# A new order for the token mixer of a hybrid encoder block: contiguous weight loads, projections between the transposes, scan constants after the norms, the Fourier work two rounds earlier, and another last filler

## The chip, the cores and the metric

The kernel runs on one core of a Trainium2 chip. The metric is the device time of one launch in microseconds (us). Engines are named as the profile names them: PE is TensorE (matmuls; PEld its weight loads), DVE is VectorE, ACT is ScalarE, POOL is GpSimd, SP is SyncE, which here only issues DMAs.

## The reference

One encoder layer on x of 512 positions by 1024, all in float32:

```python
h = rmsnorm(x, norm1_g)
z = h @ w_in                                  # 512 x 1024
# columns 0..511: S5 group, 32 channel groups of 16, 64 complex states, scans forward and backward
y = s5_scan(u, fwd) + s5_scan(u, bwd, reverse=True) + ssm_d * u
y = gelu(y);  y_ssm = y * sigmoid(y @ w_glu)
# columns 512..1023: Fourier group, 4 groups of 128 channels
f = real(fft2(f, axes=(positions, channels), norm="ortho"));  y_fno = einsum("sgc,gcd->sgd", f, w_fourier)
x = x + concat(y_ssm, y_fno) @ w_out
h = rmsnorm(x, norm2_g)
x = x + peer_ffn(h, w_query, sub_keys, expert_u, expert_v)   # 8 heads, 128 x 128 experts, top 16
out = rmsnorm(x, final_g)
```

The change touches the first half, the token mixer (the lines down to `x + concat @ w_out`), and the layout of w_query.

## The kernel before, in words

The instructions of each engine run in the order in which the program writes them (a hand-written schedule); engines wait for each other by semaphores, and a tile with `bufs=n` can be written again only when its n-th predecessor has been read. Float32 products are made as three matmuls of split operands (`mm3`: high x high, high x low, low x high). `split` makes the two parts: ACT copies the high part (line 108, tiles `whi`, `hTh`, `ygh`), DVE or POOL subtracts it to get the low part (line 109, `wlo`, `hTl`, `ygl`).

The mixer has three stretches.

- **Front.** x is loaded as four row tiles `xt`, each is normed (`normed`: square and sum on ACT, root, reciprocal and scaling on DVE, line 151), transposed on PE and split into `hTh` and `hTl` (`turned_parts`). w_in is loaded in eight column blocks of 512 KB (`w_raw`), three buffers deep. `zT(zp[q], w[q], columns)` makes the projection of S5 channel block q, `z_fourier(g, …)` that of Fourier block g. At the same time DVE, ACT and POOL build the scan constants: rotation tables by doubling (`turns(m)`, a complex product `cmul` of six operations; m = 5 is on POOL), powers `pw`, and from them `pi`, `pv`, `kap` and `ck`.
- **Loop of rounds.** The S5 group has eight blocks n of four channel groups. Block n needs, in this order: `weights_in(n)` (POOL, tile `win`), `turned_in(n)` (PE transposes, line 419), `weights_out(n)` (DVE tile `v`, ACT copies `bb`, `rc`, `sg` from `rot`), `kernels(n)` (PE, line 431), `toeplitz(n)` (DMA there and back), `states_in(n)` (PE), `scan(n)` (DVE, eight operations that end in tile `sx`) and `states_out(n)` (PE, lines 495 and 497). Round n of `for n in range(7)` scans block n on DVE while PE does filler: the Fourier projections `z_fourier` in rounds 0 to 3, then the Fourier transform (`columns`, `table`, `rows`) one round behind the other, so that `rows(i, c)`, 12 matmuls of 512 columns each, fills rounds 4 to 6.
- **Tail.** After the loop `scan(7)` runs on DVE beside a last filler on PE, `rows(3, 0)` and `rows(3, 1)`, 24 matmuls. Then come `states_out(7)`, the GLU product (`glu`), the product with w_out (`wo_part(i, k)`: row tile i, block k of the mix; blocks 4 to 7 are the Fourier half), its eight weight blocks loaded in turn through the three `raw` buffers, norm2 and the transposes for the query stage, which starts at about 266 us of the span.

From there PE is busy almost without a gap to the end, so a shift of the mixer's end shifts the end of the kernel.

Of the kernel before, what the change touches and what calls it, by code (L numbers as in the profile page):

```python
# [22 lines left out]
TC = 8  # L23
# [45 lines left out]
def build(ctx, tc, A, dbg=None, stop=None):  # L69
# [215 lines left out]
    def turns(m, gs, eng=None):  # L285
# [6 lines left out]
    for m in range(1, 5):  # L292
        turns(m, slice(0, G))
    for h in range(2):
        gs = slice(h * G // 2, (h + 1) * G // 2)
        turns(5, gs, ge)
    pw = sp.tile([128, 2, TC + 1, G], FT, name="pw")
    ve.memset(pw[:, 0, 0], 1.0)
    ve.memset(pw[:, 1, 0], 0.0)
# [9 lines left out]
    zp = [acc_bank() for _ in range(4)]  # L309
    w = []  # L310
    for i in range(NT):
        normed(xt[i], xt[i], g1, sw.tile([128, D], mybir.dt.bfloat16, tag="cm", name="scr"))
        if i:
            turned_parts(xt[i - 1], hTh, hTl, i - 1)
            w.append(w_parts(raws[i - 1], ge))
    se.activation(warm, eps, AF.Gelu)
    for q in range(2):
        zT(zp[q], w[q], slice(0, 256))


# [15 lines left out]
    pv = sc.tile([128, 3, TC + 1, G], FT, name="pv")  # L336
    for c, (src, sign) in enumerate(((0, 1.0), (1, -1.0), (0, -1.0))):
        se.activation(pv[0:64, c], pw[0:64, src], AF.Copy, scale=sign)
        se.activation(pv[64:128, c], pw[64:128, src, ::-1], AF.Copy, scale=sign)
# [12 lines left out]
    ck = sc.tile([128, 2, G, CG], FT, name="ck")  # L352
    shp = [128, G, CG]
    cmul(ck[:, 0], ck[:, 1], cre, cim, bc(kap[:, 0, :, None], shp), bc(kap[:, 1, :, None], shp), shp)
    pro.close()
# [257 lines left out]

    for n in range(7):
        if n % 2 == 0 and n < 6:
            inputs(n // 2 + 1)
        if n == 2:
            fourier_load()
        if n == 3:
            table_load(0)  # L620
            table_load(1)
        if n == 0:
            z_fourier(0, w, range(0, 4))
# [4 lines left out]
        if n < 2:  # L628
            raws.append(w_raw(6 + n))
        if n + 2 < 8:  # L630
            weights_in(n + 2)
        if 0 < n < 3:
            z_fourier(n, w, range(0, 4))
        elif n == 3:
            z_fourier(n, w, range(0, KD))
# [4 lines left out]
        elif n:  # L640
            rows(n - 4, 0)
# [4 lines left out]
        if n > 3:  # L646
            table(n - 3, 0)
        if n < 3:
            z_fourier(n, w, range(4, 8))
            w = w_parts(raws[n + 1])  # L650
        elif n > 3:
            rows(n - 4, 1)
            table(n - 3, 1)
            if n < 6:
                table_load(n - 2)
        if n >= 3:
            columns(n - 3)
        if n == 3:
            table(0, 0)
            table(0, 1)  # L660
# [21 lines left out]
    def wo_raw(k):  # L682
        raw = blk.tile([128, 1024], FT, tag="raw", bufs=3, name="raw")
        nc.sync.dma_start(raw, A["w_out"][k * 128:(k + 1) * 128])
        return raw
# [627 lines left out]
```

## Time and profile before

| | us |
|---|---|
| median of three timed runs | 1533.1 (1532.39 to 1537.7) |
| profiled execution, its own time | 1530.49 |
| span of that execution | 1528.7 |
| PE busy in the span | 1462.2 (96%) |
| DVE, ACT, POOL busy | 1288.4, 719.1, 819.2 |
| mean granted TensorE clock | 0.990 |

The span runs from the first to the last instruction of the core. A granted clock of 1 stands for 2.4 GHz, 0.5 for 1.2 GHz. In the rows below an instruction is named by its line, its engine, the tile that it writes, an arrow and the tiles that it reads; "x8" says that a row stands for eight of them in a run, and a bracket gives the engine's idle time before it and what ended that.

### The profile page before, as it was taken

The numbers are of one execution on the slowest core, as the hardware profiler recorded it, in microseconds if no ns is written. First come the engines' busy times: TensorE is split into PE (matmuls) and PEld (weight loads), VectorE is DVE, ScalarE is ACT, GpSimd is POOL, SyncE is SP. The second block draws the span as 40 slices with busy tenths as digits, with TensorE's granted clock in tenths as the row PEclk, the third lists the DMA queues.
The fourth block names the chain that finished last, engine by engine and source line by source line (L and its number), as shares of the span: only waits on it lengthen the run. The fifth ranks groups of instructions, "written<-read, shape, count | busy, mean of one in ns | idle before, by whom it ended". The sixth has DMA issues, their size and how long they took to land.

```text
span 1528.7 us, 22444 instructions
## 1 busy us (share of the span) xinstructions
PE 1462.2 (96%) x8045; PEld 1320.9 (86%) x8045; DVE 1288.4 (84%) x2156; ACT 719.1 (47%) x1332; POOL 819.2 (54%) x482
## 2 busy tenths in 40 slices
PE   1799999999998999999999999999999999999997
PEld 1678878889998999999999888888888888888885
DVE  7889744799999999988773997888888888889886
ACT  5245544334445777777773433333333333333333
POOL 5446722336795776777775544544544454444530
PEclk9899999999998999999999999999999999999999
DMA  6233353323585999999999888898888888998883
GB/s 139 69 94 84 114 175 86 97 83 124 182 297 194 327 333 295 328 327 334 329 329 357 319 293 306 326 335 323 308 306 320 321 298 318 332 337 309 299 298 111
DMA packets 205951, 388.13 MB, mean 254 GB/s; under 512 B 27152, under 2 KB 127248, under 8 KB 205712
## 3 DMA queue, kind: packets, MB, share of 16 engines
q1 hardware_dynamic: 102896, 209.86, 40.8%
q0 software_dynamic: 36864, 134.23, 24.7%
q10 hardware_dynamic: 66080, 42.61, 8.7%
q8 instruction: 63, 1.03, 0.3%
q14 instruction: 48, 0.39, 0.1%
HBM read 341.46 MB, written 45.19 MB: 253 GB/s over the span
## 4 chain that ended last, share of the span: by engine, by line
PE 78%; DVE 10%; DMA 3%; ACT 3%; issue 2%; POOL 1%; ACTq 1%; SPq 0%; POOLq 0%; DVEq 0%
PE mm L103 10%; PE mm L101 10%; PE mm L102 10%; PE acc L103 9%; PE acc L102 9%; PE acc L101 9%; PE acc L1092 5%; PE misc L103 4%; PE misc L101 4%; PE misc L102 4%; DVE one L1018 1%; PE mm L431 1%; ACT hot L1078 1%; PE misc L1180 1%; DMA gd<-stg 1%
## 5 line engine op out<-in xcount | busy, mean ns | idle before, releaser
L109 POOL TENSOR_TENSOR wlo<-raw,whi 128x1024 fp32r<-128x1024 f32 x153 | 388.3, 2540 | 511.8 <-ACT whi L108 470.9
L108 ACT ACTIVATE whi<-raw 128x1024 fp32r<-128x1024 f32 x288 | 304.6, 1059 | 345.4 <-PE misc L103 201.9
L101 PE MATMUL mm<-h2h,whi 128*128 128x384 f32 (+2 forms) x1168 | 403.1, 345 | 0.2 <-ACT h2h L163 0.2
L103 PE MATMUL mm<-h2h,wlo 128*128 128x384 f32 (+2 forms) x1168 | 396.6, 340 | 0.4 <-POOL wlo L109 0.4
L102 PE MATMUL mm<-h2l,whi 128*128 128x384 f32 (+2 forms) x1168 | 396.3, 339 | 0.3 <-DVE h2l L164 0.3
L838 DVE TENSOR_TENSOR pre<-pre,gb 128x384 f32<-128x384 f32 x128 | 182.5, 1426 | 53.2 <-ACT pre L888 24.6
L101 PEld LDWEIGHTS mm<-h2h,whi 128*128 128x128 f32 x1168 | 220.6, 189 | 5.8 <-ACT h2h L163 0.5
L102 PEld LDWEIGHTS mm<-h2l,whi 128*128 128x128 f32 x1168 | 220.6, 189 | 5.9 <-DVE h2l L164 0.5
L103 PEld LDWEIGHTS mm<-h2h,wlo 128*128 128x128 f32 x1168 | 220.1, 188 | 5.2 <-POOL wlo L109 0.8
L109 DVE TENSOR_TENSOR wlo<-raw,whi 128x1024 fp32r<-128x1024 f32 x135 | 169.9, 1258 | 55.2 <-ACT whi L108 54.2
L101 PE MATMUL acc<-whi,ah 128*128 128x512 f32 x512 | 199.4, 389 | 1.4 <-ACT ah L108 1.4
L102 PE MATMUL acc<-wlo,ah 128*128 128x512 f32 x512 | 200.2, 391 | 0.4 <-DVE wlo L109 0.3
L103 PE MATMUL acc<-whi,al 128*128 128x512 f32 x512 | 200.3, 391 | 0.0
L1144 POOL DMA_INDIRECT row<-in_expert_v_dram,ei x128 | 171.5, 1340 | 40.1 <-issue 18.2
L1154 DVE SCALAR_TENSOR_TENSOR gscr<-row,hnat 128x1024 bf16<-128x1024 f32 x128 | 183.7, 1435 | 6.0 <-DMA row<-in_expert_u_dram,ei 5.0
L1162 DVE SCALAR_TENSOR_TENSOR x<-row,pr,x 128x1024 f32<-128x1024 f32 x128 | 184.7, 1443 | 1.3
L1144 POOL DMA_INDIRECT row<-in_expert_u_dram,ei x128 | 163.5, 1277 | 29.4 <-issue 17.0
L888 ACT ACTIVATE pre<-mm 128x384 f32<-128x384 f32 x128 | 62.3, 487 | 185.9 <-PE mm L103 182.4
L1066 DVE TENSOR_TENSOR hot<-iota,tT 128x1024 f32<-128x1024 f32 x96 | 113.6, 1215 | 29.2 <-PE acc L1092 20.7
L1078 ACT ACTIVATE hot<-hot,tT 128x128 f32<-128x128 f32 x384 | 117.8, 390 | 0.0
L101 PEld LDWEIGHTS acc<-whi,ah 128*128 128x128 f32 x512 | 96.2, 188 | 21.1 <-ACT ah L108 2.1
L103 PEld LDWEIGHTS acc<-whi,al 128*128 128x128 f32 x512 | 96.1, 188 | 20.8 <-DVE al L109 0.8
(308 smaller groups left out, 2207.5 us busy)
## 6 DMA issues: line engine op xcount, KB each, us to landing
raw<-in_expert_uT_dram SPq DMA_DIRECT2D x128, 512.0 KB
raw<-in_expert_v_dram SPq DMA_DIRECT2D x128, 512.0 KB
gd<-stg ACTq DMA_DIRECT2D x24, 1024.0 KB
gb<-gd SPq DMA_DIRECT2D x64, 384.0 KB
pre_d<-pre ACTq DMA_DIRECT2D x78, 192.0 KB
pre<-pre_d SPq DMA_DIRECT2D x78, 192.0 KB
raw<-in_w_query_dram SPq DMA_DIRECT2D x16, 512.0 KB
raw<-in_w_in_dram SPq DMA_DIRECT2D x8, 512.0 KB
```

Of the source, the lines that this page charges most:

```text
L101: te.matmul(ps, lhsT=ah, rhs=bh, start=first, stop=False)
L102: te.matmul(ps, lhsT=ah, rhs=bl, start=False, stop=False)
L103: te.matmul(ps, lhsT=al, rhs=bh, start=False, stop=last)
L108: se.activation(hi, raw, AF.Copy)
L109: ins = (eng or ve).tensor_tensor(lo, raw, hi.bitcast(FT), OP.subtract)
L838: ve.tensor_tensor(pt, pt, gb[:, :, b % IG], OP.mult)
L1066: ve.tensor_tensor(hot, bc(iota[:, None, None, :128], shp), bc(tT[:, 0:2, t0:t0 + 4, None], shp), OP.is_equal)
L1078: se.activation(hot[:, 0, a], hot[:, 0, a], AF.Copy, scale=tT[:, 2, t0 + a:t0 + a + 1])
L1092: te.matmul(ps[:, a * 128:(a + 1) * 128], lhsT=hot[:, 1, a], rhs=hot[:, 0, a], start=True, stop=True)
L1144: ge.indirect_dma_start(out=row[:, :], out_offset=None, in_=A[table], in_offset=bass.IndirectOffsetOnAxis(ap=ei[:, m:m + 1], axis=0))
L1154: ve.scalar_tensor_tensor(scr, rows.pop(n), 1.0, hnat, op0=OP.mult, op1=OP.mult, accum_out=pr[:, m:m + 1])
L1162: ve.scalar_tensor_tensor(x[i], rows.pop(n), pr[:, m:m + 1], x[i], op0=OP.mult, op1=OP.add)
```

## The change

The order of the mixer is written anew; what is computed stays.

- **Loads.** `blocks()` lays out w_in and w_query on the host so that a column block is contiguous: 4 KB in a row per partition where it was eight pieces of 512 B. norm1_g, which was broadcast by DMA to 128 partitions (512 KB), is loaded as one row of 4 KB and spread by two PE matmuls with a row of ones into two PSUM banks `gb1`; `norm1(i)` scales in two halves of 512 from there. The order of the first loads changes, ssm_b moves ahead of the third block.
- **Front.** The seeds of `rot` are copied by POOL (12 copies) where ACT did it. The square's scratch tile has the tag `tm`, not `cm`, which the rotations on DVE use too. Ahead of the norms only `turns(1)` and `turns(2)` are left; `turns(3)`, `ck`, `turns(4)`, `pv` come after the fourth transposes, and POOL's `turns(5)` in two halves behind `weights_in(0)` and `weights_in(1)`, where it ran at 15 to 34 us. The projections stand between transposes.
- **Loop.** `z_fourier(0)` is done whole ahead of the loop, 1 and 2 in round 0, 3 in round 1; `columns`, `table` and `rows` stand two rounds earlier, so that `rows` fills rounds 2 to 5. Round 6 has no Fourier filler; the splits of the Fourier result (`mfh`, `mfl`) and the loads of w_out blocks 4 and 5 are there now.
- **Tail.** The last filler, ahead of `states_out(7)`, is `wo_part` of blocks 4 and 5 for row tiles 0 and 1, 24 matmuls as well.

```diff
     def w_raw(c):
         raw = blk.tile([128, 1024], FT, tag="raw", bufs=3, name="raw")
-        nc.sync.dma_start(raw.rearrange("p (k c) -> p k c", k=KD),
-                          A["w_in"][:, c * 128:(c + 1) * 128].rearrange("(k p) c -> p k c", p=128))
+        nc.sync.dma_start(raw, A["w_in"][c])
...
+    gb1 = [mm_bank() for _ in range(2)]
+    for f in range(2):
+        te.matmul(gb1[f], lhsT=g1[:, D:], rhs=g1[:, f * 512:(f + 1) * 512], start=True, stop=True)
...
-            se.activation(rot[:, c, :, 2 ** m], csn[:, c, 1 + m], AF.Copy)
+            ge.tensor_copy(rot[:, c, :, 2 ** m], csn[:, c, 1 + m])
...
+    def norm1(i):
+        r = rstd_of(sumsq(xt[i], sw.tile([128, D], mybir.dt.bfloat16, tag="tm", name="scr")))
+        for f in range(2):
+            fs = slice(f * 512, (f + 1) * 512)
+            ve.scalar_tensor_tensor(xt[i][:, fs], xt[i][:, fs], r, gb1[f], op0=OP.mult, op1=OP.mult)
...
+    norm1(0)
+    norm1(1)
+    turn1(0)
+    w = [w_parts(raws[0], ge)]
+    powers()
+    turn1(1)
+    norm1(2)
+    w.append(w_parts(raws[1], ge))
+    zT(zp[0], w[0], h0)
...
+    weights_in(0)
+    w.append(w_parts(raws[3]))
+    raws.append(w_raw(4))
+    inputs(0)
+    zT(zp[1], w[1], h1)
+    z_ssm(1, zp[1])
+    turns(3)
+    shp = [128, G, CG]
+    cmul(ck[:, 0], ck[:, 1], cre, cim, bc(kap[:, 0, :, None], shp), bc(kap[:, 1, :, None], shp), shp)
...
+    turns(4)
+    pro.close()
+    turns(5, slice(0, G // 2), ge)
+    zT(zp[2], w[2])
+    w.append(w_parts(raws[4]))
...
     kernels(0)
     toeplitz(0)
+    z_fourier(0, w[4], range(0, KD))
+    turns(5, slice(G // 2, G), ge)
     weights_out(1)
...
+        if n == 0:
+            z_fourier(1, w[5], range(0, KD))
+        elif n == 1:
+            z_fourier(3, w[7], range(0, KD))
...
+        elif n < 6:
+            rows(n - 2, 0)
...
         if n == 6:
+            for g in range(4):
...
+                se.activation(h, fstate["acc"][g], AF.Copy)
+                ve.tensor_tensor(l, fstate["acc"][g], h.bitcast(FT), OP.subtract)
...
+            wr = {k: wo_raw(k) for k in (4, 5)}
...
     scan(7)
-    wr = {k: wo_raw(k) for k in (4, 5)}
     wo = {k: wo_parts(wr[k], ge) for k in (4, 5)}
-    rows(3, 0)
-    rows(3, 1)
-    fac = fstate["acc"]
+    po = {i: [acc_bank() for _ in range(2)] for i in range(2)}
+    for k in (4, 5):
+        for i in range(2):
+            wo_part(i, k, k == 4, False)
```

POOL, from the constants to the first input weights. Before, `turns(5)` (`gm` and `rot`, here its last two operations) and the zeroing of small tiles stand ahead of the low parts of w_in and of `win`:

```order
L222 TENSOR_TENSOR rot<-rot 128x16x31
L223 TENSOR_TENSOR rot<-gm,rot 128x16x31
L303 MEMSET bb_229 128x384
L303 MEMSET bb_230 128x384
L306 MEMSET us_233 128x8
L307 MEMSET us_233 128x8
L306 MEMSET us_234 128x8
L307 MEMSET us_234 128x8
L109 TENSOR_TENSOR wlo<-raw,whi 128x1024 x3
L384 TENSOR_TENSOR win<-ssm_b,pi 128x1024
```

The same place on POOL in the changed kernel:

```order
L109 TENSOR_TENSOR wlo<-raw,whi 128x1024 x3
L399 TENSOR_TENSOR win<-ssm_b,pi 128x1024
L400 TENSOR_TENSOR gm<-ssm_b,pi 128x1024
L401 TENSOR_TENSOR win<-win,gm 128x1024
L217 TENSOR_TENSOR gm<-rot 128x496
L218 TENSOR_TENSOR rot<-rot 128x16x31
L219 TENSOR_TENSOR rot<-gm,rot 128x16x31
L220 TENSOR_TENSOR gm<-rot 128x496
L221 TENSOR_TENSOR rot<-rot 128x16x31
L222 TENSOR_TENSOR rot<-gm,rot 128x16x31
```

The first half of `turns(5)` has moved behind the first `win`; the second half stands behind the second `win` in the same way.

DVE, from the constants to the first output weights. Before, `ck` is followed by the low part of a w_in block (`wlo`) and block 0's `v`:

```order
L222 TENSOR_TENSOR ck<-ssm_c,kap 128x512
L223 TENSOR_TENSOR ck<-cm,ck 128x512
L109 TENSOR_TENSOR wlo<-raw,whi 128x1024
L384 TENSOR_TENSOR v<-ck,pv 128x1152
L385 TENSOR_TENSOR cm<-ck,pv 128x1152
L386 TENSOR_TENSOR v<-v,cm 128x1152
L109 TENSOR_TENSOR wlo<-raw,whi 128x1024
L436 TENSOR_TENSOR kf<-kf 16x4x16
```

The same place on DVE in the changed kernel:

```order
L222 TENSOR_TENSOR ck<-cm,ck 128x512
L217 TENSOR_TENSOR cm<-rot 128x480
L218 TENSOR_TENSOR rot<-rot 128x32x15
L219 TENSOR_TENSOR rot<-cm,rot 128x32x15
L220 TENSOR_TENSOR cm<-rot 128x480
L221 TENSOR_TENSOR rot<-rot 128x32x15
L222 TENSOR_TENSOR rot<-cm,rot 128x32x15
L109 TENSOR_TENSOR wlo<-raw,whi 128x1024
L399 TENSOR_TENSOR v<-ck,pv 128x1152
L400 TENSOR_TENSOR cm<-ck,pv 128x1152
L401 TENSOR_TENSOR v<-v,cm 128x1152
L109 TENSOR_TENSOR wlo<-raw,whi 128x1024
```

The six operations of `turns(4)` (and, ahead of `ck`, those of `turns(3)`) now stand between the fourth norm and block 0's `v`.

PE, behind the loop. Before, the last matmuls of `rows(3, 1)` (they read the DFT table `tbh`, `tbl`) and the first of `states_out(7)`:

```order
L101 MATMUL acc<-tbh,pqh 128x512
L102 MATMUL acc<-tbl,pqh 128x512
L103 MATMUL acc<-tbh,pql 128x512
L495 MATMUL misc<-us_234,toep 128x64
L497 MATMUL misc<-sx,v 128x64 x2
```

The same place on PE in the changed kernel:

```order
L101 MATMUL acc<-whi,mfh 128x512
L102 MATMUL acc<-wlo,mfh 128x512
L103 MATMUL acc<-whi,mfl 128x512
L510 MATMUL misc<-us_209,toep 128x64
L512 MATMUL misc<-sx,v 128x64 x2
```

The filler ahead of `states_out(7)` now reads `whi` and `wlo` of w_out blocks 4 and 5 and the split Fourier result.

## Rows read from the trace of the kernel before

**Rows 1.** Waits of PE in 0 to 262 us: releaser, total, times, longest.
```profile
PE misc L160 <- DVE rstd L136: 21.5, 1, 21.5
PE acc L103 <- DVE wlo L109: 11.3, 2, 8.3
PE acc L103 <- POOL wlo L109: 5.4, 1, 5.4
```

**Rows 2.** Nine stretches of 0 to 262 us together: busy time by engine.
```profile
sum 262.00, PE 215.66 PEld 183.82 DVE 190.54 ACT 118.49 POOL 122.62; mean PE 23.96 PEld 20.42 DVE 21.17 ACT 13.17 POOL 13.62
```

**Rows 3.** Chain that ended last: start us, duration us, piece.
```profile
152.11 0.45 PE misc L497 x4
...
153.68 0.23 PE acc L102
...
166.14 0.45 PE misc L497 x4
...
189.60 0.70 PE misc L497 x4
...
226.67 2.37 POOL wlo L109
...
249.38 1.39 DVE x L897 x2
```

**Rows 4.** Timeline of ACT at the start: start us, us, instruction, idle before.
```profile
7.81 1.57 ACT L282 ACTIVATE rot<-csn 128x32 f32<-128x32 f32 x12
...
17.93 1.06 ACT L141 ACTIVATE scr<-xt 128x1024 bf16<-128x1024 f32 x1 [7.03 <-DVE rot L223]
```

**Rows 5.** Timeline of PE: eight transposes early, and eight later.
```profile
21.49 1.94 PE L160 MATMUL misc<-ident,xt 128*128 128x128 f32 x8 [21.49 <-DVE rstd L136]
...
45.23 1.03 PE L160 MATMUL misc<-ident,xt 128*128 128x128 f32 x8
```

**Rows 6.** Timeline of DVE beside POOL, and after it.
```profile
34.75 2.36 DVE L223 TENSOR_TENSOR pw<-cm,pw 128x32 f32<-128x32 f32 x1
...
41.83 0.23 DVE L220 TENSOR_TENSOR pw<-cm,pw 128x64 f32<-128x64 f32 x1
```

**Rows 7.** Timeline of POOL before and in that stretch.
```profile
19.16 1.15 POOL L220 TENSOR_TENSOR rot<-gm,rot 128x496 f32<-128x496 f32 x1
...
34.73 6.99 POOL L109 TENSOR_TENSOR wlo<-raw,whi 128x1024 fp32r<-128x1024 f32 x3
```

**Rows 8.** Timeline of DVE, operations that are moved.
```profile
14.56 0.66 DVE L220 TENSOR_TENSOR rot<-cm,rot 128x480 f32<-128x480 f32 x1
...
51.30 0.18 DVE L344 TENSOR_SCALAR num<-pw 128x32 f32<-128x32 f32 x1
...
57.27 0.22 DVE L351 TENSOR_TENSOR kap<-kap,den 128x64 f32<-128x64 f32 x1
57.53 0.69 DVE L218 TENSOR_TENSOR cm<-ssm_c,kap 128x512 f32<-128x512 f32 x1
...
72.12 1.22 DVE L109 TENSOR_TENSOR wlo<-raw,whi 128x1024 fp32r<-128x1024 f32 x1
...
79.03 1.34 DVE L384 TENSOR_TENSOR v<-ck,pv 128x1152 f32<-128x1152 f32 x1
...
82.95 0.68 DVE L475 TENSOR_TENSOR tm<-misc,rot 128x512 f32<-128x512 f32 x1
...
88.36 0.69 DVE L485 TENSOR_TENSOR sx<-tm,misc 64x512 f32<-64x512 f32 x1
```

**Rows 9.** Timeline of POOL at the end of the loop.
```profile
180.00 2.55 POOL L109 TENSOR_TENSOR wgl<-raw,wgh 128x512 fp32r<-128x512 f32 x2 [2.62 <-ACT wgh L108]
182.50 3.79 POOL L109 TENSOR_TENSOR ygl<-zc,ygh 128x512 fp32r<-128x512 f32 x3
186.26 4.64 POOL L109 TENSOR_TENSOR wlo<-raw,whi 128x1024 fp32r<-128x1024 f32 x2
```

**Rows 10.** Timeline of ACT behind the loop.
```profile
191.11 2.07 ACT L720 ACTIVATE mfh<-acc 128x512 fp32r<-128x512 f32 x4 [0.40 <-ACT ys L499]
```

More of the change, by code (lines that the diff above doesn't have):

```diff
@@ L290, in turns @@
              bc(rot[:, 0, gs, n:n + 1], shp), bc(rot[:, 1, gs, n:n + 1], shp), shp, eng=eng)
[L292 to L296, printed above, removed]
+    turns(1)
+    turns(2)
     pw = sp.tile([128, 2, TC + 1, G], FT, name="pw")
-    ve.memset(pw[:, 0, 0], 1.0)
-    ve.memset(pw[:, 1, 0], 0.0)
+    ge.memset(pw[:, 0, 0], 1.0)
+    ge.memset(pw[:, 1, 0], 0.0)
     GQ = 4
@@ L351, in build @@
     ve.tensor_tensor(kap, kap, bc(den[:, 0:1], [128, 2, G]), OP.mult)
[L352 to L355, printed above, removed]
+    z_ssm(0, zp[0])
     fT = []
@@ L612, in glu_input, with wo_raw, wo_parts, wo_part @@
         yp.append((h, l))
+    def wo_raw(k):
+        raw = blk.tile([128, 1024], FT, tag="raw", bufs=3, name="raw")
+        nc.sync.dma_start(raw, A["w_out"][k * 128:(k + 1) * 128])
+        return raw
+    def wo_parts(raw, eng, pool=None):
+        h, l = ((pool or blk).tile([128, 1024], FR, tag=t, bufs=4 if pool else 3, name=t) for t in ("whi", "wlo"))
+        split(raw, None, h, l, eng)
+        return h, l
+    def wo_part(i, k, first, last):
+        cs = slice(i * 128, (i + 1) * 128)
+        for f in range(2):
+            fs = slice(f * 512, (f + 1) * 512)
+            mm3(po[i][f], mix[k][0][:, cs], mix[k][1][:, cs], wo[k][0][:, fs], wo[k][1][:, fs], first, last)
     for n in range(7):
@@ L645, in build @@
             weights_out(n + 2)
[L646 to L658, printed above, removed]
+        if 1 < n < 5:
+            table(n - 1, 0)
+        if n == 0:
+            z_fourier(2, w[6], range(0, KD))
+            w.append(w_parts(raws[7]))
+            table_load(0)
+        elif 1 < n < 6:
+            rows(n - 2, 1)
+            if n < 5:
+                table(n - 1, 1)
+                if n < 4:
+                    table_load(n)
+        if 0 < n < 5:
+            columns(n - 1)
+        if n == 1:
+            table_load(1)
             table(0, 0)
@@ L678, in build @@
         states_out(n)
[L682 to L685, printed above, removed]
-    def wo_parts(raw, eng, pool=None):
-        h, l = ((pool or blk).tile([128, 1024], FR, tag=t, bufs=4 if pool else 3, name=t) for t in ("whi", "wlo"))
-        split(raw, None, h, l, eng)
-        return h, l
     scan(7)
-    wr = {k: wo_raw(k) for k in (4, 5)}
     wo = {k: wo_parts(wr[k], ge) for k in (4, 5)}
-    rows(3, 0)
-    rows(3, 1)
-    fac = fstate["acc"]
+    po = {i: [acc_bank() for _ in range(2)] for i in range(2)}
+    for k in (4, 5):
+        for i in range(2):
+            wo_part(i, k, k == 4, False)
     ga = [mm_bank(), mm_bank()]
@@ L716, in build @@
     glu((2, 3), range(3))
-    for g in range(4):
-        h = fpl.tile([128, S], FR, tag=f"fTh{g}", name="mfh")
-        l = fpl.tile([128, S], FR, tag=f"fTl{g}", name="mfl")
-        se.activation(h, fac[g], AF.Copy)
-        ve.tensor_tensor(l, fac[g], h.bitcast(FT), OP.subtract)
-        mix[4 + g] = (h, l)
     wr = {k: wo_raw(k) for k in (6, 7)}
```

122 lines of the change are left out of this document (54 added, 68 removed).

## The prediction

> **What bounds the kernel now.** The first view to read is the list of what PE waited for. In the first 262 us, the mixer, it has three large entries and few small ones: 21.5 us for the first norm, 11.3 us in two waits for a low part of w_in that DVE makes, 5.4 us for one that POOL makes [rows 1]. The table of stretches adds that PE is busy 215.66 of these 262 us, DVE 190.54 [rows 2]: PE idles 46 us, almost all of it in the front, and nothing else in the mixer is a wall. The chain that ended last then says which work carries the time behind the front: it runs through PE's `states_out` of each round (they end at 152.56, 166.59 and, for block 7, 190.30), leaves PE after block 7 for loads and POOL's split of the last w_out blocks, and ends the mixer at 249.4 [rows 3]. So three things decide: when the rounds reach their PE-bound pace, how long the last rounds take, and how the tail hangs on block 7. A `rows` matmul takes 0.23 us in this chain [rows 3], 24 of them 5.6 us.
>
> The timelines show two prices that an order must pay. Beside a running POOL tensor operation, DVE's operations on two SBUF tiles take as long as the POOL operation: 2.36 us for a product of 128x32, beside POOL's three low parts of 2.33 us each, and 0.23 us for a larger one when POOL was done [rows 6, 7]. And PE at the half clock takes 1.94 us for eight transposes that take 1.03 us later [rows 5]; it starts at the half level after each long wait.
>
> **The start.** ACT's first square began at 17.93 after 7.03 us in which it waited for DVE's rotations, because of the shared scratch tag [rows 4]; ACT was free at 10.90, and the 1.57 us of seed copies leave it [rows 4], so it can begin at 9.3, 8.6 us sooner. The transposes move from 21.49 [rows 5] to about 12.9. What bounds this: x must have landed (at worst nothing is gained), and `turns(1)` and `turns(2)` wait for POOL's 12 seed copies ahead of the norm on DVE. No copy of that shape on POOL is in the trace; the nearest operation is a 128x496 product at 1.15 us [rows 7], so the copies cost between 0 and 13.8 us. I take 0.3 us each, near the bottom, for a tile a fifteenth as large; the upper end takes the whole 8.6 us back. The two PE matmuls for `gb1` lie in PE's idle start and cost nothing; without that cover they cost what two 512-column matmuls at half clock do, some 1 us (estimate, four times 0.23). Contiguous loads I count at nothing: after the scratch tag is gone ACT's own start, not x, ends the wait; a landing 1 us later costs 1 us. The projections then take the same matmuls, and PE keeps about 8 to 10 us of lead until `states_in(0)`, at about 55 us by this count.
>
> **The middle of the front.** Now DVE is late. After the fourth transposes (about 36.7) it owes `kap`, 6.2 us before, of which 51.30 to 55.9 stood beside POOL's `win` [rows 8]. In the new order `win` is again beside it, and begins at about the same moment, so that its three operations and the rest of `kap` end at about 44.5. Then come a `wlo` of 1.22 us, `turns(3)` (about 2 us, half of `turns(4)`), `ck` with six operations of 0.69 us, `turns(4)` with six of 0.66 us [rows 8]: about 55.4. Then a `wlo` and the three operations of `v` (1.34 us each) [rows 8], 5.2 us, and exactly there POOL begins the first half of `turns(5)`, six operations of about 1.1 us [rows 7], since it waits for `turns(4)`. Four alternations add 3 us or so: `v` is there at 63.6. PE has been waiting for it since 54.9, 8.7 us, and restarts at half clock, which costs 2.6 us more on 24 matmuls by the two levels [rows 3, 5]. `kernels(0)` and `z_fourier(0)` are then done at about 74.
>
> A second wait follows. Block 1's `v` meets the second half of `turns(5)` in the same way, then comes the scan, 82.95 to 89.05 or 6.1 us before [rows 8], and only behind it on DVE the `wlo` that PE needs for `z_fourier(2)`: 6.4 us of PE wait and again a cold start. Also queued behind: ACT's copy `sg` of `rot` waits for `turns(5)`, and with it the high part of the next w_in block. By this count `states_out(1)` ends at 117.7. I call this time E. With no collision at all the same count gives 108; with PE never waiting, its own work gives 99. These are the ends of this term.
>
> At this point the Trainium skill bears on the sum (SBUF — State Buffer, "SBUF: two separate sides"): it says that VectorE and GpSimd share one pair of ports as an exclusive lock, and that a VectorE operation with two SBUF inputs is blocked for the whole of a GpSimd operation that reads SBUF. This trace agrees, with 2.36 us for 0.23 [rows 6]. By the rule E is 117.7, without it 108; it speaks against `turns(5)` in its new place.
>
> **The rounds.** Rounds 2 to 4 now hold what rounds 4 to 6 held, and one of those took 14.03 us (152.56 to 166.59) [rows 3]. Round 5 has `rows` but no `columns`: 12.6. Together 54.9 us, PE-bound in both kernels, so hidden work on the other engines costs nothing here.
>
> **Round 6 and the last filler.** Before, block 7's `states_out` ended 23.7 us after block 5's (166.59 to 190.30) [rows 3], with 48 `rows` matmuls, 11.2 us, as cover. Now round 6 has no Fourier filler, and the last filler can't start before the splits of w_out blocks 4 and 5. These come last on POOL: before, POOL made `wgl` from 180.00, `ygl`, then the two `wlo` from 186.26 to 190.9 [rows 9], that is up to 24.3 us after block 5. Now `yT` needn't wait behind `columns` on DVE, but 2.07 us of `mfh` [rows 10] stand ahead of `wgh` on ACT; I get `wgl` from +8.9 in place of +13.4, `ygl` done at +15.2, the `wlo` at +17.6 and +20.0. PE idles from about +6.8, starts at half clock, and 24 filler matmuls (5.2 and 2.8 us) and then `states_out(7)` (2.7) end at +28.3, though block 7's scan is done at about +16. So 4.6 us are lost; if POOL starts at +13.4 as before, 9; if the filler were not in front, `states_out(7)` would end at +19, a gain of 4.7.
>
> **The tail.** Everything behind block 7 hangs on its store and on loads queued after it, down to POOL's last split, which ended at 229.04, 38.7 us after block 7 [rows 3]. Before, the mixer ended 59.1 us after block 7. PE has 5.6 us less to do there, but by that chain only part arrives: I take 2.3, between 0 and 5.6, nearer the half because PE waited for that split before.
>
> **The sum.** Mixer end = E + 54.9 + 28.3 + 56.8 = 117.7 + 140 = 257.7, against 249.4: 8.3 us later. The w_query loads in long runs may remove a wait below half a us. So +8 us, break-even at E = 109.2. The profiled execution took 1530.49, which gives 1538.5; the median of 1533.1 gives 1541. I forecast **1539**, about 0.4% slower than the median. The difference of the two bases, 2.6 us, is itself a third of the 0.5% (7.7 us) that a measurement of this kernel can tell from no change.
>
> **The rivals.**
> - Given back (the forecast): the lead of the front is used up by waits for `v`, `wlo` and the last filler; +3 to +11 us, 1536 to 1544. For it: the collisions are in the rows, and the split of w_out stands last on POOL. Chance 0.37.
> - Collisions mild: POOL and DVE fall beside each other less, E about 108: 108 + 140 = 248, -1 us, 1530 to 1535. For it: 10 us of lead at the start is a firm gain. Against it: `turns(5)` starts when `turns(4)` ends, and `v` is next on DVE. Chance 0.21.
> - The other side: PE never waits at `kernels(0)`. It decides whether `v` of block 0 is there before PE reaches 55. Then E is 99 to 102, the mixer ends at 239 to 242, -7.5 to -10 us, 1523 to 1526; if the last filler didn't hold up block 7 as well, up to -17. For it: PE's work in the mixer is the same, and 46 us of idle time [rows 2] is much to win from. Against it: the DVE sum above is 8 us too long for it. Chance 0.28.
> - Worse: the seed copies on POOL or the loads take back the start and both cold starts stay; E about 124, +15 us, 1548. Chance 0.14.
>
> The third holds most of "faster" (0.24 of 0.28). "Same" has the second, half of the first, and the rest of the third: 0.42. "Slower" has the other half of the first and the fourth: 0.34. The range 1520 to 1549 leaves out the far ends of the third and fourth, about 0.15 together; the forecast's own range is 1536 to 1544.
>
> **What would show it.** In the changed profile: transposes from about 13 us (right start) or 20 (copies or loads late); a PE wait of 5 to 9 us before `kernels(0)` with `v` beside POOL's `gm`; DVE's `v` operations at 2 us and more there; a second wait for a `wlo` in round 0; rounds 2 to 4 at 14.0 us each; PE's wait for POOL's `wlo` ahead of the last filler, and `states_out(7)` 28 us after `states_out(5)`. The forecast is wrong if block 0's `v` is ready before PE asks for it, if the w_out split is done when block 7's scan ends, or if the last split of the tail comes much earlier than 38 us after block 7.

## The result, and the profile after

The changed kernel takes 1543.82 us (median of 8 runs, 1538.8 to 1549.28) beside 1534.93 for the kernel before (8 runs on the same chips): a ratio of 1.006, 95% interval 1.0039 to 1.0081. It is 0.6% slower. Its profiled execution has a span of 1539.2 us against 1528.7, and the last addition to x in the mixer, which began at 249.38 [rows 3], begins at 258.44: 9.06 us later. This place, called the mixer's end below, is compared between kernels throughout.

What PE waited for in the first 275 us of the changed kernel (releaser, total, times, longest), against [rows 1]:

```profile
PE mm L446 <- DVE v L401: 10.0, 2, 8.9
PE acc L102 <- DVE hTl L164: 7.2, 2, 6.9
PE acc L101 <- ACT whi L108: 6.7, 3, 5.1
PE acc L102 <- POOL wlo L109: 5.9, 2, 3.9
PE misc L160 <- DVE xt L316: 5.1, 1, 5.1
PE acc L103 <- DVE wlo L109: 4.4, 1, 4.4
```

The single wait of 21.5 us at the start is gone and six groups of smaller ones stand in its place: for the first normed rows, for the low part of the second row tile (`hTl`), for `v` of block 0, for a low part of w_in, and two at the very end, for the high and the low part of w_out block 4. The timeline of PE has the longest of each (start, duration, instruction, idle time before it):

```profile
12.13 1.94 PE L160 MATMUL misc<-ident,xt 128*128 128x128 f32 x8 [5.14 <-DVE xt L316]
...
24.13 0.58 PE L102 MATMUL acc<-hTl,whi 128*128 128x256 f32 x1 [6.88 <-DVE hTl L164]
...
63.44 3.93 PE L446 MATMUL mm<-v,bb 128*48 128x144 f32 x16 [8.89 <-DVE v L401]
...
87.92 0.80 PE L103 MATMUL acc<-hTh,wlo 128*128 128x512 f32 x1 [4.39 <-DVE wlo L109]
...
185.42 0.80 PE L101 MATMUL acc<-whi,mfh 128*128 128x512 f32 x1 [5.14 <-ACT whi L108]
190.17 0.79 PE L102 MATMUL acc<-wlo,mfh 128*128 128x512 f32 x1 [3.95 <-POOL wlo L109]
```

The first transposes come 9.36 us sooner than before [rows 5], and the 512-column matmuls right after the last three of these waits last 0.8 us, twice their usual 0.40: PE restarts at the lower of its two clocks there. The chain that ended last gives the ends of `states_out` (blocks 1, 2, 5 and 7; these rows answer to [rows 3]) and the last split of the tail:

```profile
114.06 0.45 PE misc L512 x4
...
128.34 0.45 PE misc L512 x4
...
168.99 0.46 PE misc L512 x4
...
199.39 0.46 PE misc L512 x4
...
233.10 2.36 POOL wlo L109
```

Blocks 1 and 2 end at 114.51 and 128.79, block 5 at 169.45 and block 7 at 199.85; before, blocks 5 and 7 ended at 166.59 and 190.30. So the kernel is 2.9 us behind when round 5 is done, although it started 9.4 us ahead, and loses 6.7 more in round 6 and the last filler.

Why `v` was late is seen on DVE and POOL side by side. DVE:

```profile
56.77 2.19 DVE L399 TENSOR_TENSOR v<-ck,pv 128x1152 f32<-128x1152 f32 x1
58.89 2.29 DVE L400 TENSOR_TENSOR cm<-ck,pv 128x1152 f32<-128x1152 f32 x1
...
61.22 2.08 DVE L401 TENSOR_TENSOR v<-v,cm 128x1152 f32<-128x1152 f32 x1
```

and POOL at the same time, in the first half of `turns(5)`:

```profile
55.80 1.95 POOL L218 TENSOR_TENSOR rot<-rot 128x496 f32<-128x496 f32 x1 [1.28 <-DVE rot L222]
57.83 2.13 POOL L219 TENSOR_TENSOR rot<-gm,rot 128x496 f32<-128x496 f32 x1
59.93 2.15 POOL L220 TENSOR_TENSOR gm<-rot 128x496 f32<-128x496 f32 x1
```

Both engines are slowed: `v`'s operations take 2.1 to 2.3 us where they took 1.34 [rows 8], POOL's 2 to 2.15 where they took 1.15 [rows 7]. They take turns. That is 2.5 us of the wait of 8.9 (`v` takes 6.5 us in place of 4.0); the rest is the work that stands ahead of `v` on DVE.

The start of round 6's chain (the chain of waits), from the store of block 5's result:

```profile
169.88 4.64 DMA yd<-ys
174.54 2.98 DMA yT<-yd
...
181.63 2.50 POOL wgl L109 x2
```

The result of block 5 goes to DRAM and back in 7.6 us before the gelu and the splits can start, and the four `mfh` stand ahead of `wgh` on ACT, so POOL begins its series 12.2 us after block 5; in [rows 9] it began at 180.00, 13.4 us after. The scan of block 7 stands behind the splits as well, on DVE (ACT, then DVE):

```profile
178.98 2.06 ACT L716 ACTIVATE mfh<-acc 128x512 fp32r<-128x512 f32 x4
```
```profile
179.61 2.48 DVE L717 TENSOR_TENSOR mfl<-acc,mfh 128x512 fp32r<-128x512 f32 x4 [1.32 <-ACT mfh L716]
182.01 0.68 DVE L490 TENSOR_TENSOR tm<-misc,rot 128x512 f32<-128x512 f32 x1
```

In the stretch from 170 to 200 us PE is busy only 18.73 us and its granted clock is 0.72; before, it was 28.98 us and 0.94 (changed, then before; columns: busy time and instructions of PE, PEld, DVE, ACT, POOL, clock, DMA share, GB/s):

```profile
170.00:200.00 30.00, 18.73 (x125) 16.27 (x124) 14.48 (x22) 10.06 (x20) 11.26 (x8) 0.72 0.27 83
```
```profile
170.00:200.00 30.00, 28.98 (x184) 24.75 (x183) 14.11 (x22) 13.08 (x24) 13.49 (x9) 0.94 0.45 134
```

### The profile page after: what moved, and what is told of

It reads as the page before. It is cut to its first block, busy times and chain, and to the rows that moved or that the text cites. A ratio compares the mean times of both kernels' runs of the same rounds, so it can differ in the third digit from the quotient of the medians.

```text
span 1539.2 us, 22454 instructions
## 1 busy us (share of the span) xinstructions
PE 1469.8 (95%) x8049; PEld 1325.3 (86%) x8049; DVE 1299.5 (84%) x2159; ACT 717.6 (47%) x1320; POOL 832.7 (54%) x496
## 4 chain that ended last, share of the span: by engine, by line
PE 73%; DVE 19%; issue 3%; DMA 2%; ACT 1%; POOL 1%; SPq 0%; ACTq 0%; DVEq 0%; POOLq 0%
PE mm L101 9%; PE mm L103 9%; PE mm L102 9%; PE acc L102 9%; PE acc L103 9%; PE acc L101 9%; PE misc L101 4%; PE misc L102 4%; PE misc L103 4%; PE acc L1116 3%; DVE gscr L1178 3%; DVE hot L1090 3%; DVE one L1042 2%; DVE eid L1044 1%; DVE cide L1017 1%
## 5 line engine op out<-in xcount | busy, mean ns | idle before, releaser
L862 DVE TENSOR_TENSOR pre<-pre,gb 128x384 f32<-128x384 f32 x128 | 188.1, 1470 | 50.1 <-ACT pre L912 24.6
L109 DVE TENSOR_TENSOR wlo<-raw,whi 128x1024 fp32r<-128x1024 f32 x135 | 166.8, 1235 | 69.9 <-ACT whi L108 68.8
L1178 DVE SCALAR_TENSOR_TENSOR gscr<-row,hnat 128x1024 bf16<-128x1024 f32 x128 | 187.0, 1461 | 5.9 <-DMA row<-in_expert_u_dram,ei 4.9
L1186 DVE SCALAR_TENSOR_TENSOR x<-row,pr,x 128x1024 f32<-128x1024 f32 x128 | 185.8, 1451 | 1.3
L1168 POOL DMA_INDIRECT row<-in_expert_u_dram,ei x128 | 170.3, 1330 | 29.3 <-issue 17.6
L102 PEld LDWEIGHTS acc<-wlo,ah 128*128 128x128 f32 x512 | 96.1, 188 | 19.9 <-DVE wlo L109 0.7
```

The lines of the kernel that those rows point to most:

```text
L102: te.matmul(ps, lhsT=ah, rhs=bl, start=False, stop=False)
L109: ins = (eng or ve).tensor_tensor(lo, raw, hi.bitcast(FT), OP.subtract)
L862: ve.tensor_tensor(pt, pt, gb[:, :, b % IG], OP.mult)
L1168: ge.indirect_dma_start(out=row[:, :], out_offset=None, in_=A[table], in_offset=bass.IndirectOffsetOnAxis(ap=ei[:, m:m + 1], axis=0))
L1178: ve.scalar_tensor_tensor(scr, rows.pop(n), 1.0, hnat, op0=OP.mult, op1=OP.mult, accum_out=pr[:, m:m + 1])
L1186: ve.scalar_tensor_tensor(x[i], rows.pop(n), pr[:, m:m + 1], x[i], op0=OP.mult, op1=OP.add)
```

## The experiments

Each kernel was timed in five rounds beside the kernel before on the same chip. The table puts them together; `states_out` ends are read from the copy ACT makes of each result, which starts within 0.05 us of them where nothing holds ACT.

| kernel | states_out(1) | states_out(5) | states_out(7) | mixer's end | median us | ratio to before (95%) |
|---|---|---|---|---|---|---|
| before | 109.8 | 166.6 | 190.3 | 249.4 | 1534.9 | 1 |
| changed | 114.5 | 169.5 | 199.9 | 258.4 | 1543.8 | 1.006 (1.0039 to 1.0081) |
| e1_out7_first | 114.6 | 169.5 | 194.1 | 253.0 | 1538.0 | 1.0029 (1.0012 to 1.0047) |
| e2_v0_early | 111.0 | 165.9 | 197.1 | 254.3 | 1540.4 | 1.0044 (1.003 to 1.0059) |
| e3_no_turns5 | 120.3 | 175.2 | 206.1 | 263.5 | 1546.9 | 1.0069 (1.0051 to 1.0088) |
| e4_old_layout | 115.0 | 169.9 | 201.1 | 257.4 | 1546.8 | 1.0083 (1.0067 to 1.0099) |
| e5_constants_early | 116.2 | 171.1 | 201.6 | 260.0 | 1546.4 | 1.0084 (1.006 to 1.0108) |
| e6_const_out7 | 117.1 | 172.1 | 197.0 | 256.0 | 1543.8 | 1.0049 (1.0028 to 1.007) |
| e7_const_out7_late | 107.4 | 166.2 | 191.5 | 251.4 | 1538.7 | 1.0026 (1.0009 to 1.0043) |
| e8_out7_late | 105.8 | 164.6 | 189.9 | 248.7 | 1535.9 | 1.001 (0.9989 to 1.0031) |
| e9_front_order | 111.7 | 169.2 | 199.9 | 256.6 | 1543.8 | 1.0062 (1.0041 to 1.0082) |
| e10_best | 88.1 for block 0, 101.3 | 160.5 | 185.8 | 244.9 | 1531.3 | 0.9984 (0.9966 to 1.0003) |
| e11_split_later | 101.1 | 160.3 | 183.6 | 243.6 | 1528.8 | 0.9972 (0.9954 to 0.9991) |
| e12_quarters | 102.6 | 162.6 | 185.9 | 245.7 | 1531.2 | 0.9985 (0.9965 to 1.0004) |

The mixer's end, subtracted from the median, leaves 1283 to 1290 us in all fourteen kernels: what happens in the mixer passes to the end, and the rest varies by up to 6 us from one kernel to another. So the medians tell steps of a few us only roughly; the times inside the mixer are of one execution each. They repeat well where nothing was edited: up to block 6 the trace of `e1_out7_first` lies within 0.15 us of the changed kernel's.

**States_out(7) ahead of the last filler.** The prediction's theory: the filler's splits hold block 7.

```diff
     scan(7)
     wo = {k: wo_parts(wr[k], ge) for k in (4, 5)}
     po = {i: [acc_bank() for _ in range(2)] for i in range(2)}
-    for k in (4, 5):
-        for i in range(2):
-            wo_part(i, k, k == 4, False)
...
     states_out(7)
     states_load(7, fp, "ash")
+    for k in (4, 5):
+        for i in range(2):
+            wo_part(i, k, k == 4, False)
```

> The changed kernel with one edit: states_out(7) stands ahead of the 24 matmuls of wo_part, not behind them. Theory (the last filler holds block 7): the scan of block 7 is done at 188.7 in the changed kernel, so states_out(7) ends at about 192 in place of 199.9, the store, the loads of x and of w_out behind it come 8 us earlier, and the mixer ends 6 to 8 us earlier: 1536 to 1538 for a changed kernel of 1543.8. Rival (the tail hangs on ACT's and POOL's splits or on the loads' own length): block 7 earlier, but the mixer's end within 2 us of the changed kernel's.

PE then waits only for the scan of block 7 (timeline of PE):

```profile
188.75 0.66 PE L510 MATMUL misc<-us,toep 128*128 128x64 f32 x2 [8.39 <-DVE sx L500]
```

Block 7 ends 5.7 us sooner, not 8, because `states_out` itself now runs at the lower clock after the wait (0.66 us for a pair that takes 0.4), and the mixer's end is 5.4 us sooner. The theory holds, though not in full size, and the rival falls: the last filler is the largest part of the loss, 5.4 of 9.1 us by these two traces. Some 2.3 us of that are a stretch at the lower clock in the changed kernel's tail, which `e4_old_layout`, with the same order there, does not have (see the tail below).

**Block 0's v ahead of turns(3) and turns(4).**

```diff
-    turns(3)
     shp = [128, G, CG]
     cmul(ck[:, 0], ck[:, 1], cre, cim, ...)
...
-    turns(4)
+    weights_v(0)
+    w.append(w_parts(raws[4]))
+    turns(3)
+    turns(4)
     pro.close()
     turns(5, slice(0, G // 2), ge)
     zT(zp[2], w[2])
-    w.append(w_parts(raws[4]))
```

> The changed kernel with block 0's v and the low part of w_in block 4 ahead of turns(3) and turns(4) on DVE; nothing else moves. Theory A (the order of the constants): v is there at about 53 in place of 63.3, PE's wait of 8.9 us goes, and states_out(1), at 114.5 in the changed kernel, comes 8 us or more earlier: about -8 us. Theory B (DVE's operations on two SBUF tiles and POOL's operations exclude each other, so from 36 to 90 us the two are one engine with 56 us of work, and its order changes little): the wait at kernels(0) goes, but turns(5) starts later, the second win comes no earlier, PE waits there, and states_out(1) comes 0 to 4 us earlier.

The wait at `kernels(0)` is gone; PE waits for the second `win` instead, which POOL makes after `turns(5)`. PE's and POOL's timeline:

```profile
72.97 1.97 PE L442 MATMUL mm<-ident,win 128*128 128x128 f32 x8 [11.41 <-POOL win L401]
```
```profile
57.41 1.34 POOL L217 TENSOR_TENSOR gm<-rot 128x496 f32<-128x496 f32 x1 [15.78 <-DVE rot L219]
```

POOL stood idle for 15.78 us until `turns(4)` was there, with the second `win` queued behind. `v` itself is there at 52.1, as theory A said, but `states_out(1)` is 3.6 us sooner, which is what theory B said, and not 8.

**Turns(5) left out.** Its two calls are taken away and the columns zeroed at the start, so this kernel leaves out a part of the rotation table.

```diff
+    ge.memset(rot[:, :, :, 33:64], 0.0)
...
-    turns(5, slice(0, G // 2), ge)
...
-    turns(5, slice(G // 2, G), ge)
```

> The changed kernel with turns(5) left out: its columns of rot are zeroed at the start, so the S5 half is computed with a wrong table; 12 POOL operations of 1.1 us go. Theory A (order): only the alternations beside v go, 2.9 us for block 0 and 2 for block 1, so states_out(1) is 3 to 5 us earlier. Theory B (one engine): 13 us of the shared work go, states_out(1) is 9 us or more earlier, 103 to 105, and the second win is there 10 us earlier; the kernel takes 1532 to 1536.

Both theories fall, in sign: with 13 us of POOL work less, `states_out(1)` is 5.7 us later. POOL now goes on to the second `win` at once, and its three operations, twice as long as those of `turns(5)`, stand beside `turns(4)` on DVE. DVE, then POOL, then the wait of PE for `v`:

```profile
51.96 2.49 DVE L218 TENSOR_TENSOR rot<-rot 128x480 f32<-128x480 f32 x1
54.48 2.35 DVE L219 TENSOR_TENSOR rot<-cm,rot 128x480 f32<-128x480 f32 x1
```
```profile
51.42 2.51 POOL L400 TENSOR_TENSOR win<-ssm_b,pi 128x1024 f32<-128x1024 f32 x1
53.89 2.42 POOL L401 TENSOR_TENSOR gm<-ssm_b,pi 128x1024 f32<-128x1024 f32 x1
```
```profile
66.01 4.05 PE L447 MATMUL mm<-v,bb 128*48 128x144 f32 x16 [11.20 <-DVE v L402]
```

An operation of 0.66 us [rows 8] takes 2.4 beside one of 2.4, and `v` of block 0 is there at 65.9 in place of 63.3; the third `win` then meets `v` of block 1 in the same way, 85.1 in place of 80.6. So it is not the sum of the two engines' work that counts here: in these rows each DVE operation on two SBUF tiles ends only after the POOL operation that has begun. What that costs depends on how long the POOL operations beside DVE's chain are and on how many DVE operations they stop. The Trainium skill says as much of one operation (SBUF — State Buffer, "SBUF: two separate sides": whichever engine starts first has the shared ports for the whole instruction); what it means for an order is in these rows: taking short POOL work away let long POOL work in.

**The old layout of w_in and w_query.** In the changed kernel:

```diff
-        nc.sync.dma_start(raw, A["w_in"][c])
+        nc.sync.dma_start(raw.rearrange("p (k c) -> p k c", k=KD),
+                          A["w_in"][:, c * 128:(c + 1) * 128].rearrange("(k p) c -> p k c", p=128))
```

> The changed kernel with w_in and w_query laid out and loaded as before, in pieces of 512 B. Theory (long runs are worth nothing, since the scratch tag and the seeds set the start): first transposes at 12.1 as in the changed kernel, time within 2 us. Rival (the loads set the start): first transposes and the first w_in parts 2 to 5 us later, time 2 to 5 us more.

The first transposes are at 12.25 and the mixer's end is even 1.1 us sooner, so the long runs give the front nothing, as expected. The median is 2.9 us above the changed kernel's, more than the 2 us of the theory, with intervals that overlap (1.0067 to 1.0099 and 1.0039 to 1.0081). Of the query weights' runs the trace shows one thing: a PE wait of 0.4 us for a low part of them, at 274.33, which the changed kernel hasn't. What makes the rest of the difference behind the mixer stays open.

**Constants ahead of the norms again.**

```diff
-    turns(1)
-    turns(2)
+    for m in range(1, 5):
+        turns(m)
...
     w.append(w_parts(raws[1], ge))
+    for h in range(2):
+        turns(5, slice(h * G // 2, (h + 1) * G // 2), ge)
...
-    turns(3)
...
-    turns(4)
-    turns(5, slice(0, G // 2), ge)
...
-    turns(5, slice(G // 2, G), ge)
```

> The changed kernel with the constants ahead of the norms again: turns(3) and turns(4) on DVE behind turns(2), turns(5) on POOL behind the second w_in low part, where POOL was idle for 11.2 us (22.3 to 33.5). Theory (a POOL operation costs DVE its whole length where DVE's chain of two-SBUF operations stands beside it, and little beside norms that read PSUM): the first transposes come at 16 to 18 in place of 12.1, but block 0's v at about 58 with a PE wait of 0 to 3 us in place of 8.9; states_out(1) ends at 100 to 107 in place of 114.5; 1531 to 1537. Rival (the early start is what counts, the waits behind it follow it): everything is 4 to 6 us later, 1548.

Neither came out. PE's timeline (the second row is the wait for `v` of block 1), and the busy times of 22 to 60 us here and in the changed kernel:

```profile
18.39 1.94 PE L160 MATMUL misc<-ident,xt 128*128 128x128 f32 x8 [11.25 <-DVE xt L316]
...
82.33 3.80 PE L448 MATMUL mm<-v,bb 128*48 128x144 f32 x16 [2.54 <-DVE v L403]
```
```profile
22.00:60.00 38.00, 26.98 (x156) 24.33 (x155) 36.53 (x57) 16.74 (x29) 26.62 (x18) 0.96 0.26 76
```
```profile
22.00:60.00 38.00, 29.72 (x199) 26.34 (x199) 33.23 (x57) 15.24 (x28) 14.49 (x9) 0.96 0.25 70
```

The start is 6.3 us later, the wait for block 0's `v` is gone, and `states_out(1)` is only 1.6 us later. `v` of block 0 is there at 62.8, beside 63.3 in the changed kernel: the same work on DVE stands ahead of it in either order, in front of the start or behind it. DVE is busy 36.53 and 33.23 of 38 us in that stretch, with its waits for POOL in it. The theory had `v` at 58, but `turns(5)` didn't stand beside norms only: the six operations that make `pi` from one SBUF tile are slowed by it too, 6.2 us for 1.8 (one of them here, then in the changed kernel):

```profile
38.83 1.05 DVE L350 TENSOR_SCALAR pi<-pw 64x256 f32<-64x256 f32 x1
```
```profile
27.30 0.28 DVE L348 TENSOR_SCALAR pi<-pw 64x256 f32<-64x256 f32 x1
```

`v` of block 1, beside the third `win`, is then there at 82.2, in the changed kernel at 80.6. So the order that starts 6 us sooner is 1.6 us ahead at block 1 and 1.6 at the mixer's end.

**Both edits together.** Constants early and `states_out(7)` first:

> Constants early, as in the run beside it, and states_out(7) ahead of the last filler. If front and last filler are two separate losses, their gains add: 5.4 us for the filler and 8 to 13 for the front, 1525 to 1531. If the tail hangs on something else once block 7 is earlier, it is no faster than the better of the two alone.

The last filler's gain is there with this front too (4.0 us at the mixer's end, 260.0 to 256.0, where it was 5.4); the front's gain of 8 to 13 us does not exist, and the median is that of the changed kernel, 1543.8.

**The Fourier half up one round, not two.** On top of the two edits above, and (second) on top of `states_out(7)` first alone. The splits `mfh` and `mfl` go behind the gelu's input in round 6 in the same edit:

```diff
-        if n == 0:
-            z_fourier(1, w[5], range(0, KD))
-        elif n == 1:
+        if n < 2:
+            z_fourier(n + 1, w[n + 5], range(0, KD))
+        elif n == 2:
             z_fourier(3, w[7], range(0, KD))
...
-        elif n < 6:
-            rows(n - 2, 0)
+        else:
+            rows(n - 3, 0)
...
         if n == 6:
+            glu_weights(2)
...
+            glu_input(2, ge)
             for g in range(4):
```

> As the run with constants early and states_out(7) first, with the Fourier half moved up one round and not two: z_fourier(2) in round 1, (3) in round 2, rows in rounds 3 to 6, the splits of its result at the end of round 6. Theory (round 6 without filler leaves PE idle for some 11 us that rounds 0 and 1 pay for): block 7 ends 5 to 10 us earlier than with the rounds of the change, 1519 to 1526. Rival (PE's work is the same and rounds 0 to 1 only wait, so it moves nothing): within 2 us of that kernel.

> The changed kernel with states_out(7) ahead of the last filler and the Fourier half moved up one round, not two; its front is that of the change, with turns(5) late. Theory: z_fourier(2) no longer stands in round 0 behind the late low part, so states_out(0) ends at about 89 in place of 98.6, round 6 has 11 us of cover, block 7 ends at 181 to 185 in place of 193; 1528 to 1533. Rival: the second wait only moves to the next round, and block 7 comes within 2 us of 193.

Both gain: 4.6 us at the mixer's end with early constants (256.0 to 251.4), 4.3 with the change's front (253.0 to 248.7). With the change's front `states_out(1)` ends 8.8 us sooner, because `z_fourier(2)`, its 24 matmuls and its wait for a low part, no longer stands in round 0. Of that, 4.9 us are left at block 5 and 4.3 at block 7, not 8 to 12: rounds 2 to 5 now take 58.8 us in place of 54.9, as work that left rounds 0 and 1 is done there. As the gain stands at block 5 already, it is not the splits' new place in round 6 that makes it. In front of the scan of block 7 there is this (DVE, then PE):

```profile
175.82 2.48 DVE L722 TENSOR_TENSOR mfl<-acc,mfh 128x512 fp32r<-128x512 f32 x4 [3.92 <-ACT mfh L721]
```
```profile
184.49 0.66 PE L510 MATMUL misc<-us,toep 128*128 128x64 f32 x2 [7.32 <-issue]
```

PE is out of work there in this kernel too. With the filler's place taken back, and one of the two rounds, what is left of the change ends its mixer at 248.7, where the kernel before has 249.4: the earlier start and all else together are worth 0.7 us there. Its time cannot be told from that of the kernel before (1.001, 0.9989 to 1.0031).

**The front in an order by need.**

```diff
-    turns(3)
...
+    weights_v(0)
+    w.append(w_parts(raws[4]))
+    turns(3)
     turns(4)
     pro.close()
-    turns(5, slice(0, G // 2), ge)
...
     weights_in(1)
+    turns(5, slice(0, G // 2), ge)
     zT(zp[3], w[3])
...
-    turns(5, slice(G // 2, G), ge)
...
         turned_in(n + 1)
+        if n < 2:
+            weights_sg(n)
         scan(n)
...
+        if n == 1:
+            turns(5, slice(G // 2, G), ge)
```

> The changed kernel with its front alone in another order: v of block 0 and the low part of w_in block 4 ahead of turns(3) and turns(4) on DVE, the second win ahead of the first half of turns(5) on POOL, its second half behind the fourth win, and the copies sg of blocks 0 and 1 just ahead of their scans on ACT. Theory (what PE wants first must stand first in the shared time of DVE and POOL; turns(5) is wanted only by sg): no wait of over 3 us at kernels(0) nor at the second turned_in, scan(0) starts at 72 to 76 in place of 80.5, states_out(1) ends at 102 to 108 in place of 114.5, and as nothing behind it is changed, the time falls by the same 6 to 12 us: 1532 to 1538. Rival (DVE and POOL are full from 36 to 90 us, any order gives the same sum, as constants early did): states_out(1) within 3 us of 111, the value with v early.

> The same front with the Fourier half moved up one round and states_out(7) ahead of the last filler, as in e8_out7_late. If front, rounds and last filler are separate losses, block 7 ends 6 to 12 us before 188.6, the mixer before 243, and the time is 1523 to 1530, faster than both kernels. If the front's gain is lost to DVE in round 1 and after, block 7 comes within 3 us of 188.6.

With the change's rounds the rival is right: the waits at `kernels(0)` and `turned_in(1)` are gone, but `states_out(1)` ends at 111.7, because PE now waits for the low part that `z_fourier(2)` needs (PE):

```profile
84.95 0.79 PE L103 MATMUL acc<-hTh,wlo 128*128 128x512 f32 x1 [5.07 <-DVE wlo L109]
```

Of its 2.8 us at block 1, 0.3 are left at block 5. With the rounds one later the same front is worth 4.5 us at block 1 (105.8 to 101.3) and 3.8 at the mixer's end (248.7 to 244.9). That is less than `e10_best` was expected to give: block 7 at 185.8 is not 6 to 12 us before 188.6, the mixer's end is not before 243, and the time is within noise of the kernel before (0.9966 to 1.0003). Front and rounds are not separate: here the lead of the front was kept only where PE's next work didn't ask DVE for more.

**Two steps further.** In e10 the scan of block 0 waits for ACT's copy of `rot`, and that for POOL (ACT):

```profile
76.54 0.72 ACT L413 ACTIVATE sg<-rot 128x256 f32<-128x256 f32 x2 [10.92 <-POOL rot L222]
```

The first step moves `mfh` and `mfl` behind `scan(7)`, the second also cuts the early part of `turns(5)` to a quarter of the groups:

```diff
     scan(7)
+    for g in range(4):
+        ...
+        se.activation(h, fstate["acc"][g], AF.Copy)
+        ve.tensor_tensor(l, fstate["acc"][g], h.bitcast(FT), OP.subtract)
...
-    turns(5, slice(0, G // 2), ge)
+    turns(5, slice(0, G // 4), ge)
...
+        if n == 0:
+            turns(5, slice(G // 4, G // 2), ge)
```

> As e10_best, with the splits mfh and mfl of the Fourier result behind the scan of block 7 on ACT and DVE, not ahead of it. In e8_out7_late the four mfl, 2.48 us, and the four mfh ahead of the copy ys stand before that scan, which ends at 184.4 while PE waits 7.3 us. Theory: the scan of block 7 and block 7 itself come 2 to 3 us earlier (about 180.5 for 183.2) and the mixer ends at 242 to 243 for 244.9; 1528 to 1530. Rival (the wait is for block 7's kernel coming back through DRAM, not for the scan): no change.

> As e11_split_later, with only the first quarter of the groups (all that the scans of blocks 0 and 1 read) in the early part of turns(5), six POOL operations half as long, and the second quarter behind the third win. Theory: in e10_best the scan of block 0 waited 3.3 us for the copy sg, which waited for POOL's turns(5) until 76.5; that wait goes, states_out(0) ends 2 to 4 us before 88.1 and block 7 as much earlier, the mixer at 239 to 241; 1525 to 1528. Rival (the six operations of the second quarter then stand beside the next v and take it back): states_out(1) within 1 us of e10_best's 100.6.

The first holds: PE's wait ahead of `states_out(7)` is 2 us shorter than in e10 (7.32) and block 7 ends 2.2 us sooner, the mixer 1.3.

```profile
178.18 0.66 PE L523 MATMUL misc<-us,toep 128*128 128x64 f32 x2 [5.33 <-issue]
```

At 1528.75 us, 0.9972 of the kernel before (0.9954 to 0.9991), it is 0.3% faster, by an interval that only just leaves out 1. The second does not hold: the scan of block 0 does come 1.6 us sooner, but `states_out(1)` ends 1.5 us later than without it and the mixer 2.1. Its rival named POOL beside DVE's next `v`, but those three operations lose only 0.4 us. The larger loss is on ACT: its copy `sg` for block 2 reads the quarter that was moved, waits for it, and the next high part of a weight block waits behind (ACT with the step, then without it):

```profile
89.43 0.73 ACT L413 ACTIVATE sg<-rot 128x256 f32<-128x256 f32 x2 [9.81 <-POOL rot L222]
90.06 1.04 ACT L108 ACTIVATE whi<-raw 128x1024 fp32r<-128x1024 f32 x1
```
```profile
81.14 0.70 ACT L413 ACTIVATE sg<-rot 128x256 f32<-128x256 f32 x2
81.75 1.04 ACT L108 ACTIVATE whi<-raw 128x1024 fp32r<-128x1024 f32 x1
```

## Why the prediction was right, step by step

- **The start** was given as 12.9 and is 12.13. POOL's seed copies take 1.98 us for twelve, 0.17 each, not 0.3. The two matmuls for `gb1` take 3.75 us, not 1, but PE is idle around them (they end at 7.0).
- **Block 0's v** was given at 63.6 with a wait of 8.7; it ends at 63.30 and PE waits 8.9. The mechanism is the one of the text: DVE's chain is too long, and `turns(5)` taking turns with `v` adds 2.5 us (given: 3 or so). The restart was given 2.6 us and costs about 1.8 (`kernels(0)` takes 3.93 us, 2.13 in the next round). But the reading that without those collisions `states_out(1)` would be at 108 does not stand: without `turns(5)` it is at 120.3, because other POOL work moves up.
- **The second wait** was mis-sized: 4.4 us in place of 6.4, and `states_out(1)` 114.5 in place of 117.7.
- **The rounds**: 54.9 given (its own terms, three times 14.03 and 12.6, add up to 54.7); 169.45 less 114.51 is 54.94.
- **Round 6 and the last filler**: 28.3 given, 30.4 measured. The step that was off is POOL's start, taken at 8.9 us after block 5 because `yT` no longer queues behind `columns`; it is at 12.2, since the way through DRAM takes 7.6 us and `mfh` 2.1. The filler holds block 7 as described, but by 5.7 us in the first experiment, not the 9.3 of the text (28.3 less 19): the scan of block 7 was put at 16 us after block 5 and is done at 19.3, since it stands behind `mfl` on DVE. So even without the filler block 7 ends 24.7 us after block 5, where before it was 23.7; the gain of 4.7 us that the text saw there does not exist.
- **The tail** was given a gain of 2.3 us and has 0.5 (59.1 before, 58.6 now). The last split does come 3.1 us sooner after block 7 (35.6 us for 38.7). But PE waits 1.92 us for it and restarts at the lower clock, 0.50 for 5.5 us, with matmuls of 0.63 us:

```profile
236.53 0.63 PE L101 MATMUL acc<-whi,mg 128*128 128x512 f32 x1
...
241.45 0.40 PE L101 MATMUL acc<-whi,mg 128*128 128x512 f32 x1
```

  From that split to the mixer's end it takes 23.0 us where it took 20.3. This is not the order's doing alone. `e4_old_layout` has the same order and a wait of 1.93 us, and its clock stays at 1.00 there:

```profile
237.10 0.50 PE L102 MATMUL acc<-wlo,mg 128*128 128x512 f32 x1 [1.93 <-POOL wlo L109]
```

  Its tail is 56.3 us, against 56.8 given; in `e9_front_order`, the same order again, it is 56.7, and in e2, e3 and e5 57.3 to 58.5. So the term was of the right size, and the 1.8 us that it missed here go to the clock.
- **The sum**: mixer's end 257.7 given, 258.4 measured. The terms' errors, -3.2, +2.1 and +1.8, nearly cancel, so part of the sum's closeness is luck. (The break-even was given at E = 109.2; 249.4 less 140 is 109.4.) The time, 1543.8, is 4.8 above the forecast of 1539 and at the upper edge of its own range of 1536 to 1544: the two times it was counted from differ by 2.6 us, the kernel before measured 1.8 more in the later runs, and the rest is within what the stretch behind the mixer varies.

Of the loss of 9.06 us at the mixer's end, shown by taking parts back one after the other: 5.4 us are the last filler's place (some 2.3 of them the low clock of this one trace's tail), 4.3 the Fourier half's second round, and -0.7 all the rest. The times agree in direction, 1.006, 1.0029 and 1.001 of the kernel before, but neighbouring intervals overlap and only the first and the last are clear of each other, so the size of each step rests on the traces. The early start, 9.4 us, is real and is used up by waits for DVE and POOL.

## What to carry to other kernels

An earlier start is worth what the engines that bound the next stretch can do with it: here the work on DVE ahead of block 0's `v` was the same in either order, and the order that started 6 us sooner came out 1.6 us ahead. Before moving an engine's filler to an earlier round, look at what the emptied round then waits for, and never put a filler whose operands are made last ahead of the step on which a store and a chain of loads hang. Where two engines take turns, count the operations of the one and the length of those of the other, not their sum; and before a filler is cut up, look for every copy that reads the piece that now comes late.

## What was not expected of the hardware

Taking away twelve POOL operations of 1.1 us made the kernel no faster (1546.9 us beside 1543.8) and its front 5.7 us slower: DVE operations of 0.66 us took 2.4 us beside the 2.4 us operations that moved up. Operations on one SBUF tile were stopped too: 0.28 us alone, 1.05 beside POOL's of 1.1. And the clock behind the same wait of 1.9 us in the tail differed between kernels with the same order: 0.50 for 5.5 us behind 235.5 in the changed kernel, 1.00 behind 237.1 in `e4_old_layout`.
